# A trunk kernel on one core: weight loads issued strictly in program order, job additions two chunks later, and a unit's additions written between the high and the low part of its loaded sums

## Chip, cores and metric

The kernel runs on one core of a Trainium2 chip. The metric is the device time of one execution in microseconds (us). An engine's name in a profile stands for: PE the matrix engine, PEld its weight loads, DVE VectorE, ACT ScalarE, POOL GpSimd, SP SyncE (which here only issues DMA loads).

## The reference

An encoder trunk over 256 tokens of width 2048, batch 1, float32, two layers. Layer 0 mixes tokens by neighbourhood attention with 16 heads, layer 1 by a short gated convolution; each layer ends with a gated MLP of width 5632. Cut to what matters:

```python
h = x
for i in range(2):
    a = rms_norm(h, mix_norm[i])
    mixed = neighborhood_attention(a, ...) if i == 0 else short_conv_mixer(a, ...)
    h = h + mixed
    h = h + conv_glu_ffn(rms_norm(h, ffn_norm[i]), ...)
return rms_norm(h, final_norm)

# short_conv_mixer:  gb, gc, h = split(x @ w_in);  (gb * conv3(gc * h)) @ w_out
# conv_glu_ffn:      g, u = split(conv3(x @ w_up) + b);  (silu(g) * u) @ w_down
```

Nearly all of the work is x @ w with float32 weights, about 486 MB of them read once.

## The kernel before, in words

**Float32 by parts.** Every weight is split on the chip. A *chunk* is one load of 128x1024 float32 (512 KB) into a buffer `raw` (six buffers); ACT casts it to a high part `hi` (line 179), DVE subtracts that from the chunk to get the low part `lo` (line 180), six buffers each. PE then adds up three products: high x high, high x low, low x high.

**Two kinds of phase.** In a `Phase` (the projections into heads, `wqk`; into the MLP, `wup`; into the short convolution, `wsc`) weights are the stationary operand. A work item is a *pair* of output tiles of 128 features and four chunks; PE runs 32 matmuls on `hi` (line 251, with the activations' high and low parts beside each other, 512 columns), then 32 on `lo` (line 259, 256 columns). In a `Tokens` phase (`wo`, `wdown`, `wscout`) weights are the moving operand, three matmuls to a product (lines 442 to 444), and a work item is a *unit*: a plain one, or one with seven products in the place of eight, which needs sums of weights.

**What follows a pair.** The result of a `wup` tile leaves PSUM by: ACT copy (304), DVE addition (305), DVE product with the norm factor (310), ACT first tap of a convolution (318), two DVE taps (320), for the second tile of a pair silu on ACT (724), DVE product (727), ACT cast to the high part (283) and DVE subtraction (284). After some pairs GpSimd forms sums of the activations (lines 505 to 508), which ACT and DVE split again. A `wsc` tile goes the same way with lines 699, 702 and 316 in the place of 318, 724 and 727. A `wqk` pair gives q and k of a head; its scores (lines 596 to 598), softmax (603 to 611) and the transposes of its probabilities (621) follow some items later.

**Jobs.** A unit with seven products needs two sums of weight tiles that can be had ahead of time. A *job* (`make`) in an earlier `Phase` loads three tiles of 256 KB (lines 191 to 193) into activation buffers, later adds them (DVE, lines 198 and 199), and later still stores both sums to DRAM as `kept` (ACT's DMA queue, line 204). The unit loads them back as one chunk (line 146) and makes the last two sums from them on DVE (`pair_of_sums`, lines 159 and 160); ACT and DVE split those too (179, 180). There are 66 jobs and 66 such units. The lists `S_FIRST` to `S_ATT` say which units they are, `QK_JOBS` to `SC_JOBS` how many jobs each `Phase` takes, and `Phase.__init__` puts jobs between the first eighth and three quarters of its items.

**What sets the order.** `prep_to` walks the chunks some items ahead of PE (`AHEAD` = 4 chunks) and records each chunk's load, copy and subtraction. A job's additions and stores wait in `stores` for their chunk number:

```python
stores.append((len(prepped) + 4, adds))
stores.append((len(prepped) + 7, store))
```

The program is recorded in a layer that schedules it: from the recorded program it decides, engine by engine, in which order instructions stand, by its own reckoning of when each can begin; the place in the recorded program is a priority. `issue_after(x)` makes the instructions recorded inside it stand behind `x` on their engine. The order that results is fixed in the built program.

## Time and profile before

| what | value |
|---|---|
| median of 3 runs | 2222.01 us (2215.89 to 2222.76) |
| the profiled execution's own time | 2220.94 us |
| its span, first to last instruction | 2219.1 us |
| mean granted clock of PE | 0.997 |
| busy: PE, DVE, ACT, POOL | 99%, 84%, 58%, 5% of the span |
| DMA | mean 237 GB/s |

The span is what the profile divides; 1.8 us of the execution lie around it. A busy PE is drawn from modelled ends of its matmuls, so PE's share says that there are few gaps, not that it is at its peak. The clock that the throttle grants to PE is listed for every stretch of the span.

### The profile page before, as it was taken

Reading aid. Unit: us, or ns where it says so; the run is one execution under the profiler, and the core shown is the slowest. Engines: PE = TensorE matmul, PEld = TensorE weight load, DVE = VectorE, ACT = ScalarE, POOL = GpSimd, SP = SyncE. Lnnn points to the kernel's source line nnn. Section 1 sums busy time; section 2 is a strip of 40 time slices with the busy share of each in tenths; the row PEclk is TensorE's granted clock in tenths of the full one; section 3 lists DMA queues with packets and bytes.
Section 4 is the critical chain, followed back from the end, with each engine's and each line's share of the span. In section 5 each row is a group of like instructions: output and inputs, shape, how many; then the busy total and the mean of one; then the engine's idle time right before and its main releaser. Section 6 shows DMA issues by size and latency. Waiting matters only on the chain.

```text
span 2219.1 us, 33057 instructions
## 1 busy us (share of the span) xinstructions
PE 2190.1 (99%) x11710; PEld 1887.3 (85%) x11710; DVE 1853.0 (84%) x2856; ACT 1290.4 (58%) x1991; POOL 109.0 (5%) x159
## 2 busy tenths in 40 slices
PE   9999999999999999999999999999999999999998
PEld 8888888888888888887888888878888878888886
DVE  8788778888889888788887777888788989888888
ACT  7555555666665666565564455566556556566565
POOL 1011100000000000000000010000010000000000
PEclk9999999999999999999999999999999999999999
DMA  8799647777657788766698885677876667877575
GB/s 290 252 323 296 209 158 222 259 249 248 213 185 231 232 264 256 237 198 208 211 321 283 275 273 190 198 242 252 265 248 212 199 226 248 251 249 237 160 234 157
DMA packets 347670, 524.91 MB, mean 237 GB/s; under 512 B 19824, under 2 KB 250352, under 8 KB 347504
## 3 DMA queue, kind: packets, MB, share of 16 engines
q1 hardware_dynamic: 327120, 487.55, 68.9%
q10 hardware_dynamic: 20384, 35.24, 4.2%
q8 instruction: 92, 1.51, 0.3%
q14 instruction: 74, 0.61, 0.1%
HBM read 486.01 MB, written 36.70 MB: 236 GB/s over the span
## 4 chain that ended last, share of the span: by engine, by line
PE 73%; DVE 15%; issue 5%; ACT 3%; DMA 3%; SPq 0%; POOL 0%; ACTq 0%; DVEq 0%
PE mm L251 36%; PE mm L259 19%; DVE lo L180 7%; PE mm L444 3%; PE mm L443 3%; PE mm L442 3%; ACT hi L179 3%; DVE raw L160 1%; PE mm L668 1%; PE mm L670 1%; PE mm L669 1%; DVE raw L159 1%; DVE hi L180 1%; DMA act<-in_wdown 1%; DMA raw<-in_wup 1%
## 5 line engine op out<-in xcount | busy, mean ns | idle before, releaser
L180 DVE TENSOR_TENSOR lo<-raw,hi 128x1024 fp32r<-128x1024 f32 (+1 forms) x858 | 1020.3, 1214 | 121.4 <-ACT hi L179 70.7
L179 ACT CAST hi<-raw 128x1024 fp32r<-128x1024 f32 (+1 forms) x924 | 905.1, 1009 | 371.7 <-DVE raw L160 136.2
L251 PE MATMUL mm<-a,hi 128*128 128x512 f32 x4096 | 962.9, 391 | 2.0 <-DVE a L292 0.9
L251 PEld LDWEIGHTS mm<-a,hi 128*128 128x128 f32 x4096 | 759.7, 188 | 156.0 <-DVE a L292 2.2
L259 PEld LDWEIGHTS mm<-a,lo 128*128 128x128 f32 x4096 | 513.8, 192 | 14.2 <-DVE lo L180 2.4
L259 PE MATMUL mm<-a,lo 128*128 128x256 f32 x4096 | 519.9, 283 | 2.2 <-DVE lo L180 2.2
L442 PE MATMUL mm<-hi,act 128*128 128x512 f32 x624 | 245.0, 394 | 5.3 <-DVE h L339 2.1
L444 PE MATMUL mm<-hi,act 128*128 128x512 f32 x624 | 243.8, 391 | 0.0
L318 ACT ACTIVATE conv<-pad,pt 128x256 f32<-128x256 f32 x176 | 103.0, 599 | 207.7 <-DVE pad L310 199.5
L443 PE MATMUL mm<-lo,act 128*128 128x512 f32 x564 | 220.5, 391 | 0.0
L320 DVE SCALAR_TENSOR_TENSOR conv<-pad,pt,conv 128x256 f32<-128x256 f32 x384 | 178.3, 480 | 27.3 <-ACT conv L318 20.7
L304 ACT COPY corr<-mm 128x256 f32<-128x256 f32 x256 | 90.9, 370 | 159.6 <-PE mm L259 138.1
L442 PEld LDWEIGHTS mm<-hi,act 128*128 128x128 f32 x624 | 117.6, 188 | 33.2 <-ACT hi L179 5.0
L444 PEld LDWEIGHTS mm<-hi,act 128*128 128x128 f32 x624 | 117.4, 188 | 24.3
L443 PEld LDWEIGHTS mm<-lo,act 128*128 128x128 f32 x564 | 106.4, 189 | 22.1
L305 DVE TENSOR_TENSOR corr<-mm,corr 128x256 f32<-128x256 f32 x256 | 104.7, 417 | 10.4 <-ACT corr L304 10.2
L198 DVE TENSOR_TENSOR act<-act 128x512 f32<-128x512 f32 x66 | 45.9, 695 | 67.2 <-DMA act<-in_wdown 45.2
L284 DVE TENSOR_TENSOR act<-conv,act 128x256 fp32r<-128x256 f32 x88 | 40.1, 456 | 61.0 <-ACT act L283 61.0
L442 PE MATMUL mu<-hi,sf 128*128 128x512 f32 x186 | 73.5, 395 | 7.3 <-ACT hi L179 7.3
L443 PE MATMUL mu<-lo,sf 128*128 128x512 f32 x186 | 73.4, 395 | 1.1 <-DVE lo L180 1.1
L444 PE MATMUL mu<-hi,sf 128*128 128x512 f32 x186 | 72.5, 390 | 0.0
L310 DVE TENSOR_TENSOR pad<-corr,rstd 128x256 f32<-128x256 f32 x176 | 71.8, 419 | 0.1
(160 smaller groups left out, 1573.4 us busy)
## 6 DMA issues: line engine op xcount, KB each, us to landing
raw<-in_wup SPq DMA_DIRECT2D x352, 512.0 KB, 5.1
raw<-in_wdown SPq DMA_DIRECT2D x124, 512.0 KB, 4.4
raw<-in_wsc SPq DMA_DIRECT2D x96, 512.0 KB, 5.6
act<-in_wdown SPq DMA_DIRECT2D x156, 256.0 KB, 6.2
kept<-act ACTq DMA_DIRECT2D x132, 256.0 KB, 4.9
raw<-kept SPq DMA_DIRECT2D x66, 512.0 KB, 3.8
raw<-in_wqk SPq DMA_DIRECT2D x56, 512.0 KB, 5.6
raw<-in_wv SPq DMA_DIRECT2D x32, 512.0 KB, 4.8
```

What stands on the lines that cost most here:

```text
L179: newest["ACT"] = nc.scalar.copy(out=hv, in_=r)
L180: newest["DVE"] = nc.vector.tensor_sub(out=lv, in0=r, in1=hv.bitcast(F32))
L251: nc.tensor.matmul(self.ps[ft], lhsT=prepped[i][0][:, o:o + P], rhs=self.src[k], start=k == 0, stop=False)
L259: nc.tensor.matmul(self.ps[ft][:, S:], lhsT=prepped[i][1][:, o:o + P], rhs=self.src[k][:, :S], start=False, stop=k == self.nk - 1)
L304: nc.scalar.copy(out=corr, in_=ps[:, S:])
L305: nc.vector.tensor_add(out=corr, in0=ps[:, :S], in1=corr)
L310: nc.vector.tensor_mul(out=dst, in0=both(ps), in1=rstd)
L318: nc.scalar.activation(c, x[:, 1:S + 1], AF.Identity, scale=w[1], bias=b)
L320: nc.vector.scalar_tensor_tensor(out=c, in0=x[:, tap:tap + S], scalar=w[tap], in1=c, op0=ALU.mult, op1=ALU.add)
L442: nc.tensor.matmul(ps, lhsT=xh, rhs=wh, start=start, stop=False)
L443: nc.tensor.matmul(ps, lhsT=xh, rhs=wl, start=False, stop=False)
L444: nc.tensor.matmul(ps, lhsT=xl, rhs=wh, start=False, stop=stop)
```

## The change

Every load of weights, the jobs' included, goes through a new function `load`, which puts it behind the load recorded just before it on SP. Before, only the jobs' loads stood behind an earlier load. `parts` is split, so that a unit's last two sums are recorded between the high part (ACT) and the low part (DVE) of its loaded chunk. A job's additions are due six chunks after its loads in the place of four, its stores nine in the place of seven. Jobs begin at a fifth of the items where the `Phase` has single-tile items ahead, at once elsewhere (an eighth before), and end at three quarters, in the `wsc` phase at nine tenths.

```diff
-                newest["SP"] = nc.sync.dma_start(out=raw[:, :w], in_=src)
+                load(raw[:, :w], src)
...
             if kind == "kept":
-                newest["SP"] = nc.sync.dma_start(out=raw, in_=src())
-                t13 = parts(raw)
-                prepped.append((t13, parts(pair_of_sums(raw, prepped[-1][2], prepped[-2][2]))))
+                load(raw, src())
+                t13, low = high_part(raw)
+                t24 = pair_of_sums(raw, prepped[-1][2], prepped[-2][2])
+                low()
+                prepped.append((t13, parts(t24)))
...
+    def load(out, in_):
+
+        with ExitStack() as order:
+            if "SP" in newest:
+                order.enter_context(tc.issue_after(newest["SP"].ins))
+            newest["SP"] = nc.sync.dma_start(out=out, in_=in_)
...
+    def high_part(r):
...
         newest["ACT"] = nc.scalar.copy(out=hv, in_=r)
-        newest["DVE"] = nc.vector.tensor_sub(out=lv, in0=r, in1=hv.bitcast(F32))
-        return hi, lo
+
+        def low():
+            newest["DVE"] = nc.vector.tensor_sub(out=lv, in0=r, in1=hv.bitcast(F32))
+        return (hi, lo), low
...
-        stores.append((len(prepped) + 4, adds))
-        stores.append((len(prepped) + 7, store))
+        stores.append((len(prepped) + 6, adds))
+        stores.append((len(prepped) + 9, store))
...
-            made, lo, hi = 0, len(order) // 8, len(order) * 3 // 4
+            made, lo, hi = 0, len(order) // 5 if intro else 0, int(len(order) * until)
...
-    Phase(wsc, range(3 * KT), KT, a2, sc_evac, intro=3, jobs=take(SC_JOBS))
+    Phase(wsc, range(3 * KT), KT, a2, sc_evac, intro=3, jobs=take(SC_JOBS), until=0.9)
```

The changed file's lines from 156 on are some 9 higher (179 becomes 188, 180 becomes 191, 251 becomes 260, 304 becomes 313). All engines have the same instructions in both; what moved is their order, at three places above all.

**ACT, first `wup` phase, between two pairs.** Before: the pair on PE here is `mm_4877` and `mm_4894`, and the next is `mm_4998` and `mm_5015`, which reads `hi_4974`, `hi_4980` (both some rows above this piece), `hi_4986` and `hi_4994`; `hi_5088`, `hi_5094` and `hi_5102` belong to the pair after that. `corr` is the copy of a finished tile out of PSUM.

```order
L179 CAST hi_4986<-raw_4984 128x1024
L179 CAST hi_4994<-raw_4992 128x1024
L724 ACTIVATE g_4821<-conv_4817 128x256
L179 CAST hi_5088<-raw_5086 128x1024
L283 CAST act_4848<-conv_4843 128x256
L179 CAST hi_5094<-raw_5092 128x1024
L304 COPY corr_4927<-mm_4877 128x256
L304 COPY corr_4953<-mm_4894 128x256
L318 ACTIVATE conv_4931<-pad2_85,pt_79 128x256
L179 CAST hi_5102<-raw_5100 128x1024
L318 ACTIVATE conv_4957<-pad0_83,pt_79 128x256
L724 ACTIVATE g_4935<-conv_4931 128x256
```

All four copies for the next pair, and two for the one after, stand ahead of the first row that needs this pair's matmuls. The same pair in the changed program is `mm_4864` and `mm_4881`, and the next, `mm_4985` and `mm_5002`, reads `hi_4963` first, then `hi_4969`, `hi_4975` and `hi_4981`:

```order
L313 COPY corr_4914<-mm_4864 128x256
L327 ACTIVATE conv_4918<-pad2_85,pt_79 128x256
L313 COPY corr_4940<-mm_4881 128x256
L733 ACTIVATE g_4922<-conv_4918 128x256
L327 ACTIVATE conv_4944<-pad0_83,pt_79 128x256
L292 CAST act_4949<-conv_4944 128x256
L188 CAST hi_4963<-raw_4961 128x1024
L188 CAST hi_4969<-raw_4967 128x1024
L188 CAST hi_4975<-raw_4973 128x1024
L188 CAST hi_4981<-raw_4979 128x1024
```

Now all four copies for the next pair stand behind the whole evacuation of this one, down to the cast of its last activations. Counted over both programs, the first copy that an item needs stands behind a row that needs the last matmul of the item before it in no case before, and in 45 cases now: 33 in the `wup` phases (25 of them behind the cast of the activations as here, 7 behind the casts of GpSimd's sums as well, one behind the `conv` row), 10 in the `wsc` phase (5 right behind a `corr` copy, 2 behind the cast of the activations, 3 behind GpSimd's sums as well) and 2 in `wqk`.

**PE, `wqk` phase, second and third group of heads.** `sc` are the scores of a head, `tr` the transposes of its probabilities, which need the softmax of those scores. Before:

```order
L259 MATMUL mm<-a,lo 128x256 x16
L596 MATMUL sc<-qk 128x256
L597 MATMUL sc<-qk 128x256
L598 MATMUL sc<-qk 128x256
L596 MATMUL sc<-qk 128x256
L597 MATMUL sc<-qk 128x256
L598 MATMUL sc<-qk 128x256
L259 MATMUL mm<-a,lo 128x256 x16
L251 MATMUL mm<-a,hi 128x512 x32
L259 MATMUL mm<-a,lo 128x256 x16
L621 MATMUL tr<-pt,s 128x128 x4
```

Between the scores and the transposes stand 64 matmuls of the next pair. Now:

```order
L268 MATMUL mm<-a,lo 128x256 x16
L605 MATMUL sc<-qk 128x256
L606 MATMUL sc<-qk 128x256
L607 MATMUL sc<-qk 128x256
L605 MATMUL sc<-qk 128x256
L606 MATMUL sc<-qk 128x256
L607 MATMUL sc<-qk 128x256
L630 MATMUL tr<-pt,s 128x128 x4
L260 MATMUL mm<-a,hi 128x512 x32
```

The scores follow the last matmul of their own pair, and the transposes follow the scores with nothing between.

**DVE, a unit with seven products in the first `wdown` phase.** `raw_7653` is the loaded chunk of sums, `raw_7648` the tile in which the last two sums are made. In the changed program:

```order
L191 TENSOR_TENSOR hi_7650<-raw_7648,hi_7650 128x512
L191 TENSOR_TENSOR lo_7656<-raw_7653,hi_7655 128x1024
L167 TENSOR_TENSOR raw_7648<-raw_7653,raw_7648 128x512
L168 TENSOR_TENSOR raw_7648<-raw_7648,raw_7621 128x512
L191 TENSOR_TENSOR lo_7662<-raw_7648,hi_7661 128x1024
```

Nothing moved here: before, the same five rows stand in the same order (with lines 180, 159 and 160), and the low part `lo_7656` is still ahead of both additions. Over the 66 units, the low part stands ahead of both additions in 30 before and 28 now, between them in 16 and 16, behind both in 20 and 22; 64 units keep the order that they had.

## The prediction, as it was put on record before the changed kernel ran

> **What bounds the kernel now.** I read the page's busy times first, then what PE waited for, then the groups by line with shapes kept apart, then stretches around PE's longest waits.

> ```profile
> span 2219.1 us, 33057 instructions
> ...
> PE 2190.1 (99%) x11710; PEld 1887.3 (85%) x11710; DVE 1853.0 (84%) x2856; ACT 1290.4 (58%) x1991; POOL 109.0 (5%) x159
> ```

> PE is the bound throughout: nothing done on another engine shows in the time unless it makes PE wait, and every wait put in front of PE shows in full. PE's own waits in all:

> ```profile
> PE mu L442 <- ACT hi L179: 7.9, 12, 1.5
> PE mm L259 <- DVE lo L180: 2.2, 1, 2.2
> ...
> PE mm L251 <- ACT hi L179: 0.6, 3, 0.2
> ```

> The reader is to see the last row: in the `Phase` stages, where line 251 is the first matmul of a pair, PE waited 0.6 us in all for its high parts. There is almost nothing to gain there, and something to lose. The first row belongs to the units with seven products.

> Whether ACT can be late shows in a stretch of the `wsc` phase, by its waits:

> ```profile
> DVE act L198 <- DMA act<-in_wdown: 4.1, 1, 4.1
> ACT corr L304 <- DVE act L198: 3.7, 1, 3.7
> ...
> PE mm L259 <- DVE lo L180: 2.2, 1, 2.2
> ```

> A job's addition waited 4.1 us at DVE's head for its load; a store of those sums waited on ACT for the addition, and behind the store a copy `corr` stood 3.7 us that needed only PE. Each engine takes its list in order, and what stands behind a waiting row waits too; here it ended as 2.2 us on PE. By that reading the 45 places of the order at which a pair's first high part stands behind the evacuation of the pair before are 45 waits of PE.

> **The change part by part.** *The copies behind evacuations.* The rows of the chain, in time per instruction:

> ```profile
> L251 PE MATMUL mm<-a,hi 128*128 128x512 f32 x4096 | 962.9, 391 | 2.0 <-DVE a L292 0.9 <-DVE h L339 0.6 <-ACT hi L179 0.6
> L179 ACT CAST hi<-raw 128x1024 fp32r<-128x1024 f32 x842 | 862.0, 1047 | 360.6 <-DVE raw L160 136.2 <-PE mm L251 43.7 <-PE mm L444 39.0
> L259 PE MATMUL mm<-a,lo 128*128 128x256 f32 x4096 | 519.9, 283 | 2.2 <-DVE lo L180 2.2
> ...
> L320 DVE SCALAR_TENSOR_TENSOR conv<-pad,pt,conv 128x256 f32<-128x256 f32 x384 | 178.3, 480 | 27.3 <-ACT conv L318 20.7 <-ACT conv L316 3.6
> ...
> L305 DVE TENSOR_TENSOR corr<-mm,corr 128x256 f32<-128x256 f32 x256 | 104.7, 417 | 10.4 <-ACT corr L304 10.2
> L318 ACT ACTIVATE conv<-pad,pt 128x256 f32<-128x256 f32 x176 | 103.0, 599 | 207.7 <-DVE pad L310 199.5 <-DVE corr L305 7.8
> L304 ACT COPY corr<-mm 128x256 f32<-128x256 f32 x256 | 90.9, 370 | 159.6 <-PE mm L259 138.1 <-DVE corr L305 9.4 <-DVE act L198 6.9
> ...
> L310 DVE TENSOR_TENSOR pad<-corr,rstd 128x256 f32<-128x256 f32 x176 | 71.8, 419 | 0.1
> ...
> L727 DVE TENSOR_TENSOR conv<-conv,g 128x256 f32<-128x256 f32 x88 | 37.2, 423 | 5.2
> ...
> L283 ACT CAST act<-conv 128x256 fp32r<-128x256 f32 x88 | 35.3, 401 | 12.4 <-DVE conv L727 11.8
> ...
> L507 POOL TENSOR_TENSOR s<-conv,s 128x128 f32<-128x128 f32 x27 | 16.3, 603 | 2.1
> ...
> L505 POOL TENSOR_TENSOR s<-conv 128x128 f32<-128x128 f32 x27 | 14.3, 529 | 284.3 <-DVE conv L727 284.3
> ```

> From the pair's last matmul to the next pair's first high part: copy 0.37, addition 0.42, product 0.42, tap 0.60, two taps 0.96, product 0.42, cast 0.40, copy 1.05, together 4.64 us. One tap of the pair's first tile stands among these on DVE (0.48), and some nine hand-overs from engine to engine come to about 0.3. That is 5.4 us of PE with nothing to run. A bound from above is what the same chain took before, with other rows mixed in (ACT's timeline):

> ```profile
> 463.29 0.37 ACT L304 COPY corr<-mm 128x256 f32<-128x256 f32 x1 [1.55 <-PE mm L259]
> ...
> 469.76 0.40 ACT L283 CAST act<-conv 128x256 fp32r<-128x256 f32 x1
> 470.62 1.05 ACT L179 CAST hi<-raw 128x1024 fp32r<-128x1024 f32 x1 [0.46 <-ACT act L283]
> ```

> From 463.29 to 470.16, 6.87 us, and a copy more makes 7.9. The bounds are 4.6 and 7.9; I take 5.4, as the rows that were mixed in (`hi`, `lo`) stand behind the chain now.
> - `wup`, behind the cast: 25 x 5.4 = 135.0.
> - `wup`, behind GpSimd's sums: three GpSimd rows more (about 0.55 each) less the overlap with the cast: 1.6 more, 7 x 7.0 = 49.0.
> - `wup`, behind the `conv` row: 0.37 + 0.42 + 0.42 + 0.60 + 1.05 and 0.2 for hand-overs, 3.1.
> - `wsc`, right behind a `corr` copy: 0.37 + 1.05 and hand-overs, 5 x 1.7 = 8.5; behind the cast (copy, addition, two products, cast and copy at 0.37, 3 x 0.42, 0.40 and 1.05, two taps of the tile before, less their overlap) 2 x 4.2 = 8.4; behind GpSimd's sums too, 3 x 5.8 = 17.4.
> - `wqk`: scores wait for copy, addition, product, cast and subtraction (about 2.0), run for 0.7 (six matmuls of line 259's size at 519.9 / 4096 us), and the transposes wait for the softmax, whose rows are

> ```profile
> L603 DVE SCALAR_TENSOR_TENSOR s<-sc,bias 128x256 f32<-128x256 f32 x32 | 12.8, 414 | 0.0
> ...
> L608 ACT ACTIVATE s<-s,m 128x256 f32<-128x256 f32 x32 | 16.0, 501 | 7.1 <-DVE m L606 7.1
> ...
> L611 DVE TENSOR_SCALAR s<-s,z 128x256 f32<-128x256 f32 x32 | 11.3, 394 | 0.1
> L606 DVE TENSOR_REDUCE m<-s 128x2 f32<-128x512 f32 x16 | 10.8, 675 | 0.0
> ```

> two each of the first three and one of the last, 3.3, with small rows and hand-overs about 4.3: 6.5 without the 0.7 of work and rounded, twice, 13.0.

> Sum 135.0 + 49.0 + 3.1 + 34.3 + 13.0 = 234.4 us. What PE misses then cannot be made up, as it is the bound. Within such a pair the other three copies follow at 1.05 each, while eight matmuls of line 251 take 1.9 (962.9 / 4096 each): no second wait.

> *The clock.* Stretches around two of PE's waits, PE alone: busy time, matmuls, granted clock, DMA.

> ```profile
> 1276.00:1278.30 2.30, 0.13 (x2) 1.00 0.90 279
> 1278.35:1281.77 3.42, 3.42 (x13) 0.50 1.01 244
> 1281.77:1285.20 3.43, 3.43 (x17) 1.00 0.85 306
> ...
> 1046.50:1050.00 3.50, 2.09 (x9) 1.00 0.56 152
> 1050.00:1053.40 3.40, 3.18 (x15) 1.00 0.93 280
> ```

> After 2.17 us without work the clock fell to half for 3.42 us, which costs 1.7; 1.4 us without work left it whole. So gaps of 3 us and more should each bring one such stretch: 25 + 7 + 1 + 5 + 2 = 40 gaps x 1.7 = 68.0. The five of 1.7 us lie between the two rows; I give them nothing. Per gap the bounds are 0 and 3.4 (two stretches).

> [...]

> *Jobs' additions later.* The 132 additions and 132 stores are as many as before, two chunks later on DVE and ACT. The one wait of theirs that reached PE goes: 2.2 and its half clock of 1.7, 4.0 gained. What else DVE waited for them was covered by PE's matmuls.

> *Loads in order on SP.* The same loads; a chunk's load now also waits behind a job's three loads. Cover: the loads still stand more than most of a pair ahead, and a pair is 32 rows each of lines 251 and 259, 11.6 us, against a landing of about 5 us:

> ```profile
> raw<-in_wup SPq DMA_DIRECT2D x352, 512.0 KB, 5.1
> ...
> act<-in_wdown SPq DMA_DIRECT2D x156, 256.0 KB, 6.2
> ```

> I take 0. Without the cover each of the 52 jobs in `wup` and `wsc` would add up to 6.2.

> *Additions between a unit's parts.* 64 of 66 units keep DVE's order, so the 7.9 us of the unit's waits stay: 0, with bounds of -7.9 and, as the low part could come later by two additions in two units, +2.8.

> Sum: the profiled execution's 2220.9 (span 2219.1 and 1.8 around it) + 234.4 + 68.0 - 4.0 = 2519.3; the median stands 1.1 above that execution: 2520.

> **The rivals.**
> - *Not slower: ACT does not hold the copies back.* If a high part were cast as soon as its load has landed, whatever waits ahead of it, PE would find it done, and only the 4.0 are left: 2218. It decides at whether the copy ends before the pair's last `lo` matmul does, place by place. Against it: the 3.7 us row of `corr` behind another's wait. 4%, half of it faster if the units' 7.9 go too.
> - *The waits without the clock.* If gaps that return every 11 or 22 us leave the clock whole: 2452. For it: most short gaps did; against: the 0.50 row. 10%.
> - [...] 14%.
> - *Late loads on top.* If half of the 52 jobs add 3 us, as SP stands behind job loads whose buffers come free late, 2600. For it: DMA shares near 1.0 in the stretch above; against: the gaps give loads more time. 7%.

> **How the numbers follow.** Forecast 65%, the rivals 35%. The forecast's own range is 2480 to 2565 (chain 5.0 to 5.9, clock 1.2 to 2.2 a gap). The range over the cases, 2455 to 2570, leaves out the not-slower case, most of late loads and a part of the second. A difference of 0.3%, 6.7 us, is about what this kernel's runs can tell from none: faster 0.02, same 0.02, slower 0.96.

> **What the profile after would show.** PE's waits for ACT's `hi` in the first `hi` matmul of a pair go from 0.6 us to near 215 over some 43 waits, most between 5 and 7.5 us, in the `wup` and `wsc` phases; PE's busy share near 88%; the mean clock near 0.95 to 0.975; the stretch of 0.50 after most gaps; ACT waiting much longer for DVE's `pad` and product rows; the units' row at 6 to 9 us; DVE's waits for job loads gone. Wrong would be: fewer than 40 such waits, or waits of 2 us (then the order doesn't bind as read); a whole clock; new rows of ACT waiting for `raw` loads.

## The result, and the profile after

The changed kernel takes 2540.4 us (median of 4 runs, 2538.8 to 2542.4) against 2222.1: ratio 1.144, 95% interval 1.1417 to 1.1463. The forecast was 2520, slower. The page of the profiled execution, its own time 2542.4 us:

```profile
span 2540.6 us, 32802 instructions
...
PE 2291.6 (90%) x11710; PEld 1954.9 (77%) x11710; DVE 1885.4 (74%) x2856; ACT 1308.3 (51%) x1991; POOL 95.8 (4%) x159
```

The span is 321.5 us longer. PE's busy time accounts for 101.5 of that (2291.6 against 2190.1) with the same 11710 matmuls, its idle time for 220.0. What PE waited for (us in total, times, longest):

```profile
PE mm L260 <- ACT hi L188: 214.7, 45, 6.9
PE mu L451 <- ACT hi L188: 7.0, 11, 1.5
PE tr L630 <- DVE s L620: 6.9, 2, 3.5
PE sc L605 <- ACT qk L292: 3.6, 2, 1.8
```

The first row was 0.6 us in 3 waits. Of its 45 waits now, 43 (213.9 us) are at places counted from the order; the other two, at 9.0 and 836.1 us of the span, are 0.6 and 0.2 us long and were not. The two places in `wqk` show in the rows `tr` and `sc`, so that 45 of 45 places brought a wait. In each of the 43 the copy that PE waited for began at once behind the evacuation's row: ACT did not wait for a load there. One such wait on ACT, of those behind GpSimd's sums, in the first `wup` phase (start, duration, engine, line, work, and in brackets the idle time ahead):

```profile
458.15 0.41 ACT L292 CAST act<-conv 128x256 fp32r<-128x256 f32 x1 [1.03 <-DVE conv L736]
463.65 0.37 ACT L313 COPY corr<-mm 128x256 f32<-128x256 f32 x1 [5.09 <-PE mm L268]
...
469.33 0.40 ACT L292 CAST act<-conv 128x256 fp32r<-128x256 f32 x1 [1.53 <-DVE conv L736]
470.54 0.51 ACT L292 CAST sf<-s 128x384 fp32r<-128x384 f32 x1 [0.80 <-POOL s L515]
471.07 0.30 ACT L292 CAST act<-s 128x128 fp32r<-128x128 f32 x1
471.27 3.88 ACT L188 CAST hi<-raw 128x1024 fp32r<-128x1024 f32 x4
```

and on PE:

```profile
461.54 3.99 PE L268 MATMUL mm<-a,lo 128*128 128x256 f32 x32
472.37 2.08 PE L260 MATMUL mm<-a,hi 128*128 128x512 f32 x4 [6.83 <-ACT hi L188]
```

The four `hi` copies at 471.27 are those of the next pair. Their loads had been issued from 451.33 on, and the trace has them landed by 456.4, 458.2, 459.7 and 460.9. ACT had stood idle for 5.09 us with `corr` next in its list, until PE ended the pair: time for all four copies (4 x 1.05), had they stood ahead. Over the whole kernel this is a row of ACT's groups (busy us, mean ns, then idle before and what ended it), 138.1 of the idle time before, 505.2 now:

```profile
L313 ACT COPY corr<-mm 128x256 f32<-128x256 f32 x256 | 95.2, 372 | 515.2 <-PE mm L268 505.2 <-DMA act<-in_wscout 6.7 <-DMA kept<-act 1.5
```

The other part of the loss is the clock. Stretches of 3.41 us around the same wait, PE alone (busy time, matmuls, granted clock, DMA):

```profile
463.06:466.48 3.42, 2.47 (x21) 1.00 0.17 67
466.48:469.89 3.41, 0.00 (x0) 1.00 0.00 0
469.89:473.30 3.41, 0.93 (x2) 0.50 0.00 0
473.30:476.72 3.42, 3.42 (x9) 0.50 0.52 165
476.72:480.13 3.41, 3.41 (x16) 1.00 0.89 270
```

Two stretches at half clock follow one wait, the first of them partly still idle. In the whole record of the granted clock, the last 6 us of the span left out, there are 76 such stretches, 259.4 us, in which PE is at work for 196.2. At half clock a matmul on `hi` (line 260) started 0.427 us after the one ahead of it, at full clock 0.227 (medians over the changed kernel). I count half of PE's time at work there as lost, an estimate: 98.1 us (by these two steps it would be 47%). Before it was two stretches, 6.8 us, and by the same estimate 3.4 lost.

### The profile page after: what moved, and what is told of

Read it like the earlier page. It is cut to its first block, busy times and chain, and to the rows that moved or that the text cites. A ratio compares the mean times of both kernels' runs of the same rounds, so it can differ in the third digit from the quotient of the medians.

```text
span 2540.6 us, 32802 instructions
## 1 busy us (share of the span) xinstructions
PE 2291.6 (90%) x11710; PEld 1954.9 (77%) x11710; DVE 1885.4 (74%) x2856; ACT 1308.3 (51%) x1991; POOL 95.8 (4%) x159
## 4 chain that ended last, share of the span: by engine, by line
PE 77%; DVE 11%; ACT 7%; issue 3%; DMA 1%; POOL 0%; ACTq 0%; SPq 0%; DVEq 0%
PE mm L260 40%; PE mm L268 16%; PE mm L453 4%; PE mm L452 4%; PE mm L451 4%; ACT hi L188 3%; DVE lo L191 3%; DVE conv L329 2%; ACT conv L327 1%; PE mu L452 1%; PE mu L453 1%; PE mu L451 1%; DVE corr L314 1%; PE mm L678 1%; PE mm L679 1%
## 5 line engine op out<-in xcount | busy, mean ns | idle before, releaser
L260 PE MATMUL mm<-a,hi 128*128 128x512 f32 x4096 | 1057.4, 418 | 215.7 <-ACT hi L188 214.7
L191 DVE TENSOR_TENSOR lo<-raw,hi 128x1024 fp32r<-128x1024 f32 (+1 forms) x858 | 1009.4, 1212 | 211.5 <-ACT hi L188 104.6
L260 PEld LDWEIGHTS mm<-a,hi 128*128 128x128 f32 x4096 | 823.7, 204 | 402.8 <-ACT hi L188 225.6
L188 ACT CAST hi<-raw 128x1024 fp32r<-128x1024 f32 (+1 forms) x924 | 893.3, 1010 | 325.6 <-DVE raw L168 120.4
L268 PEld LDWEIGHTS mm<-a,lo 128*128 128x128 f32 x4096 | 513.0, 191 | 11.8
L313 ACT COPY corr<-mm 128x256 f32<-128x256 f32 x256 | 95.2, 372 | 515.2 <-PE mm L268 505.2
L327 ACT ACTIVATE conv<-pad,pt 128x256 f32<-128x256 f32 x176 | 105.8, 601 | 85.6 <-DVE pad L319 85.6
L292 ACT CAST act<-conv 128x256 fp32r<-128x256 f32 x88 | 35.5, 404 | 75.2 <-DVE conv L736 75.2
## 6 DMA issues: line engine op xcount, KB each, us to landing
raw<-in_wup SPq DMA_DIRECT2D x352, 512.0 KB, 5.7
raw<-in_wdown SPq DMA_DIRECT2D x124, 512.0 KB, 4.4
raw<-in_wsc SPq DMA_DIRECT2D x96, 512.0 KB, 6.1
act<-in_wdown SPq DMA_DIRECT2D x156, 256.0 KB, 5.9
kept<-act ACTq DMA_DIRECT2D x132, 256.0 KB, 3.9
raw<-kept SPq DMA_DIRECT2D x66, 512.0 KB, 4.1
raw<-in_wqk SPq DMA_DIRECT2D x56, 512.0 KB, 6.4
raw<-in_wv SPq DMA_DIRECT2D x32, 512.0 KB, 5.7
```

The source lines that it names most:

```text
L188: newest["ACT"] = nc.scalar.copy(out=hv, in_=r)
L191: newest["DVE"] = nc.vector.tensor_sub(out=lv, in0=r, in1=hv.bitcast(F32))
L260: nc.tensor.matmul(self.ps[ft], lhsT=prepped[i][0][:, o:o + P], rhs=self.src[k], start=k == 0, stop=False)
L268: nc.tensor.matmul(self.ps[ft][:, S:], lhsT=prepped[i][1][:, o:o + P], rhs=self.src[k][:, :S], start=False, stop=k == self.nk - 1)
L313: nc.scalar.copy(out=corr, in_=ps[:, S:])
L327: nc.scalar.activation(c, x[:, 1:S + 1], AF.Identity, scale=w[1], bias=b)
```

## Experiments

Theory A: the time is lost because ACT's copies for a pair stand behind the evacuation of the pair before, which the strict order of loads brings about. Rivals: B, the later additions or moved jobs do it; C, loads in strict order are late; D, the longer busy time is not the clock.

**The strict order undone, all else kept.**

```diff
-    def load(out, in_):
+    def load(out, in_, behind=False):
-            if "SP" in newest:
+            if behind:                 # True for the jobs' loads alone
                 order.enter_context(tc.issue_after(newest["SP"].ins))
```

> The changed kernel with one part undone: loads of chunks are no longer put behind the load recorded before them (the jobs' loads still are); later additions and stores, job spacing and the split unit stay. Theory A (the loss comes from ACT's order, which the strict order of loads brings about): no copy stands behind the evacuation of the pair before, PE's waits for hi in the phases fall from 214.7 us to under 3, the clock is near 0.997, and the time is 2218 us (2222 less the 4.0 of the one wait for a job's addition). Rival B (the later additions and stores, or the moved jobs, hold ACT and DVE up): the time stays within 20 us of 2540.

2216.1 us, ratio 0.9978 (0.9969 to 0.9987). The row of PE's waits for `hi` in the phases is down to 0.4 us in 2 waits; the clock is 0.998. B falls: additions, stores, job spacing and units are those of the changed kernel here.

**The strict order alone, added to the kernel before.** The order that `load` sets, and nothing else of the change.

> The kernel before with only the strict order of loads added; additions and stores of jobs four and seven chunks after their loads, old spacing, old units. Theory A: 43 copies behind evacuations instead of 45, waits of PE for hi in the phases near 210 us, half-clock stretches as in the changed kernel, time 2535 us (2520 to 2550). Rival B: 2222 us.

2528.2 us, ratio 1.1377 (1.1357 to 1.1397).

```profile
PE mm L260 <- ACT hi L188: 211.6, 43, 7.0
```

41 of these waits stand at places counted from the order (two others, 1.2 and 0.2 us, do not); with the two places in `wqk` that makes the 43 counted. One part of the change is thus both necessary and nearly sufficient for the loss.

**In order, but not behind jobs; and behind jobs only.** Two halves of the strict order, in the changed kernel:

```diff
# not behind jobs: a job's load waits for the newest chunk load, and no load waits for it
+            x = nc.sync.dma_start(out=out, in_=in_)
+        if not job:
+            newest["SP"] = x
# behind jobs only: jobs' loads, and the first chunk load after them
-            if "SP" in newest:
+            if job or was_job[0]:
                 order.enter_context(tc.issue_after(newest["SP"].ins))
+        was_job[0] = job
```

Expected of the first:

> The changed kernel, but a chunk's load stands behind the chunk load before it only, no longer behind a job's loads; a job's loads stand behind the last chunk load as before. Theory A, narrowed (what turns ACT's order is that a chunk's load is put behind a job's loads, for whose buffers the scheduler reckons a long wait): no copy behind an evacuation, 2218 us. Rival C (any strict order of loads on SP makes loads late): over 2400 us.

and of the second:

> The changed kernel, but only the first chunk load after a job stands behind the job's loads (and the jobs' loads behind the newest load, as in both kernels); the other chunk loads are free. Theory A, narrowed (that one order brings about all 45 places): 45 places, 2540 us (2530 to 2550). Rival: the strict order of the other loads is needed too, so that the later copies slip: under 2400.

2216.1 us, ratio 0.9977 (0.9967 to 0.9986), for the first, 2537.2 us, ratio 1.1425 (1.1401 to 1.1449), for the second. The second has the same 43 waits at the counted places, 213.7 us, and the two in `wqk`. What turns ACT's order is one relation: the first chunk load after a job is put behind that job's loads. Chunk loads in strict order among themselves cost nothing.

Why this relation makes the scheduler put the copies so late is not shown: its reckoning leaves no trace. A hint is that loads wait on SP for what they hardly waited for before. Their issues waited for the landing of an earlier job's store twice before, and 75 times in the changed kernel (SP's waits, of before and of after):

```profile
SPq L141 <- DMA kept<-act: 5.9, 2, 3.2
```
```profile
SPq L161 <- DMA kept<-act: 269.9, 75, 8.6
```

**Strictly in order, with the copies forced ahead.** This keeps every load where the change put it and moves only ACT's rows.

```diff
-                    self.evac(ft, self.ps.pop(ft))
+                    later_evac.append((self.evac, ft, self.ps.pop(ft)))   # pairs of wup and wsc
...
                 prep_to(ends[item[0]] + AHEAD)
+            for evac, f, ps in later_evac:
+                evac(f, ps)            # its corr copies stand behind newest["ACT"]
```

> The changed kernel with every load strictly in order as there, but the evacuation of a pair in the wup and wsc phases is recorded after the loads and copies of the next pair, and its corr copies are made to stand behind the newest of these copies on ACT. Theory A (ACT's order, not the loads, is what costs): of the 45 places five are left, which the edit does not reach (2 in wqk at 1.8 + 3.5 us, and the three pairs that follow single tiles, 3.0 + 1.6 + 4.9): 20 us, and some 7 half-clock stretches of 1.7: 2216 + 32 = 2248 us, 2235 to 2265. Rival C (loads in strict order come late behind the jobs' loads): copies wait for loads instead, over 2300.

2243.0 us, ratio 1.0102 (1.0086 to 1.0118), forecast 2248. The five places left are there with the sizes worked out (9.3 + 6.9 + 3.6 = 19.8 us), while the loads' waits on SP for those stores are longer than in the changed kernel (PE's waits, then SP's):

```profile
PE mm L260 <- ACT hi L188: 9.3, 3, 4.9
...
PE tr L637 <- DVE s L627: 6.9, 2, 3.5
PE sc L612 <- ACT qk L296: 3.6, 2, 1.8
```
```profile
SPq L161 <- DMA kept<-act: 327.0, 92, 9.7
```

So C falls: the loads' waits for stores are there in full, and PE does not notice. What the five places leave is near: 19.8 us of waits and an estimated 8.9 of half clock (half of 17.8 us of work there), 28.7, against 26.9 over the 2216.1 of the loads undone. The rest of the loss goes with ACT's order alone.

**The waits filled with idle matmuls.** At 38 of the 43 places in the row of `hi` (all but the five right behind a `corr` copy), on PE, ahead of the pair's first matmul:

```diff
+            with tc.issue_after(last[0].ins):          # the last matmul of the pair before
+                for i in range(n):                     # n from the size of the wait
+                    newest["PE"] = nc.tensor.matmul(x, lhsT=src[0][:, :P], rhs=src[1][:, :S],
+                                                    start=i == 0, stop=i == n - 1)
```

> The changed kernel with 16 to 48 idle matmuls (256 columns, 0.12 us each, results unused) put on PE at the start of 38 of the 45 pairs that wait, sized to fill the wait but for about 1 us; ACT's and DVE's orders are those of the changed kernel. Theory A (of the 321 us lost, about 220 are waits and about 100 the half clock after them): the waits' ends do not move, but the stretches at half clock after them go; mean clock above 0.985, time 2450 us (2435 to 2465). Rival D (the 100 us of longer busy time is not the clock but matmuls that follow their copies one by one, or slower because loads crowd in): 2520 to 2545 us. If the idle matmuls push the pairs behind them: above 2545.

2456.3 us, ratio 1.1056 (1.1037 to 1.1074), clock 0.994. PE does 1412 matmuls more (the group's row below) and the kernel is 84 us faster than the changed one. What is left of the waits stands in the second row.

```profile
L235 PE MATMUL st<-a 128*128 128x256 f32 x1412 | 175.5, 283 | 0.0
```
```profile
PE mm L275 <- ACT hi L188: 45.2, 45, 1.6
```

The half-clock stretches fall from 76 to 7 (23.9 us, PE at work for 16.2), which by the same estimate is worth (196.2 - 16.2) / 2 = 90 us. The idle matmuls and what is left of the waits come to 175.5 + 45.2 = 220.7, 6.0 more than the 214.7 that they stand for, and so 84 is left of the 90. D falls: PE's busy time without the idle matmuls is 2377.0 - 175.5 = 2201.5 us, where the changed kernel has 2291.6, 90.1 more, so the longer busy time was the clock. It also shows the prediction's second rival, the waits with a whole clock, priced at 2452.

**2.2 us left idle in each wait.** The same with 1007 idle matmuls in the place of 1412.

> As e4_gaps_filled, with fewer idle matmuls (5 to 38), so that about 2.2 us of each of the 38 waits is left without work in the place of 0.9. The waits end where they did; what differs between the rules is how many of the 38 bring a stretch at half clock. If the clock counts PE's work in windows of 3.41 us that run on freely, and a window with less than about half its time at work is followed by one at half clock (as the windows of the changed kernel and of e4 read): the 2.2 us must lie with at least 1.6 of it in one window, (3.41 + 2.2 - 3.2) / 3.41 = 70%, some 27 stretches of 1.7 us on top of 2456: 2502 us, 2490 to 2512. If any wait of 2 us and more brings one: 38, 2521. [...]

2476.7 us, ratio 1.1160 (1.1138 to 1.1182), below both forecasts, and 20.4 above the 2456.3 of the waits filled. Of the 38 waits with 2.0 us idle and more (at most 2.35) 18 brought a half-clock stretch in the profiled execution, not 27 and not 38. That execution took 2483.3 us at a clock of 0.983; the other three, 2475.1 to 2477.4 at 0.986, by that clock had some fewer. Where the border lies can be read from stretches of 3.41 us that begin where the clock's own steps lie, counted in steps of 3.413 us from a recorded change of the clock. Two of them, each with the one behind it:

```profile
867.42:870.83 3.41, 1.60 (x7) 1.00 0.00 0
870.83:874.24 3.41, 3.41 (x17) 1.00 0.74 219
2161.07:2164.48 3.41, 1.54 (x7) 1.00 0.01 2
2164.48:2167.89 3.41, 3.41 (x10) 0.50 0.71 226
```

1.60 us at work kept the clock, 1.54 did not. With a border just above 1.54 at work, 1.87 idle, I estimate the share of positions in which a wait of 2.2 us brings a half stretch at (3.41 + 2.2 - 3.74) / 3.41 = 55%, 21 of 38; my 1.6 came from stretches with other matmuls in them and was too low. What I foresaw holds in kind, with the border at 45 to 47% of a stretch at work; that every wait of 2 us brings one does not.

**The later additions alone.** Six and nine chunks in the kernel before (the diff's two lines).

> The kernel before with only the jobs' additions six and stores nine chunks after their loads. Prediction's step: the one wait of 2.2 us on PE at 1278 and its half clock go, 4.0 us: 2217 us, ratio 0.998. Rival: another stretch takes the wait's place: 2221, ratio 1.000.

2218.1 us, ratio 0.9982 (0.9973 to 0.9991): 2 to 6 us gained, against the 4.0 of the prediction. (In this run and the next two a job's three loads also stand in order among themselves; the next run has that too, and its time is that of the kernel before.) The waits did not go as the prediction had it. PE's wait of 2.2 us for a low part became three:

```profile
PE mm L268 <- DVE lo L191: 3.1, 3, 1.3
```

One of the two half-clock stretches went, an estimated 1.7 us; where the rest of the gain comes from is not shown. DVE still waited for the jobs' loads, 69.5 us before and 71.4 here, nearly all in the first of a job's two additions. With the strict order alone, the additions still due after four chunks, it did not (that first addition, here and there):

```profile
L207 DVE TENSOR_TENSOR act<-act 128x512 f32<-128x512 f32 x66 | 46.1, 699 | 71.6 <-DMA act<-in_wdown 47.5 <-DMA act<-in_wscout 19.3 <-DMA act<-in_wo 4.4
```
```profile
L207 DVE TENSOR_TENSOR act<-act 128x512 f32<-128x512 f32 x66 | 45.2, 684 | 0.0
```

**A unit's additions recorded between the parts, alone.** The diff's part in the `kept` branch.

> The kernel before, with only a unit's two additions recorded between the high and the low part of its loaded sums, nothing forced. Prediction's step: 64 of 66 units keep their order on DVE, no change: ratio 1.000, 2221. Rival: the two units that change (from the low part ahead to the low part behind) are among those at which PE waits, and up to 2 x 1.7 us go: ratio 0.9985.

Ratio 0.9997 (0.9986 to 1.0008). Recorded order is only a priority here; this part does nothing that can be measured.

**The same, forced.** In all 66 units, in the kernel before:

```diff
+                with tc.issue_after(newest["sum"].ins):    # the second of the two additions
                     low()
```

> The kernel before, where the low part of a unit's loaded sums is made to stand behind both additions on DVE (in all 66 units; the changed kernel left 28 of them with the low part ahead). If the low part ahead of the additions is what makes PE wait for the high part of the last two sums: of the 7.9 us (12 waits of up to 1.5) at least 5 go, 2216 us, ratio 0.9975. Rival: the low part, 1.4 us later, is now what PE waits for (line 452 in place of 451): 2221 or up to 2.8 above.

2202.6 us, ratio 0.9918 (0.9903 to 0.9932): about 18 us by that ratio, where I had counted on 5 to 8. First the groups of the kernel before, then of this one (busy us, mean ns, idle before):

```profile
L442 PE MATMUL mm<-hi,act 128*128 128x512 f32 x624 | 245.0, 394 | 5.3 <-DVE h L339 2.1 <-ACT hi L179 2.0 <-DVE corr L305 1.0
...
L442 PE MATMUL mu<-hi,sf 128*128 128x512 f32 x186 | 73.5, 395 | 7.3 <-ACT hi L179 7.3
L443 PE MATMUL mu<-lo,sf 128*128 128x512 f32 x186 | 73.4, 395 | 1.1 <-DVE lo L180 1.1
```
```profile
L452 PE MATMUL mm<-hi,act 128*128 128x512 f32 x624 | 243.5, 391 | 0.8 <-DVE h L349 0.8
...
L453 PE MATMUL mu<-lo,sf 128*128 128x512 f32 x186 | 72.5, 390 | 0.0
...
L452 PE MATMUL mu<-hi,sf 128*128 128x512 f32 x186 | 72.3, 390 | 0.3 <-ACT hi L189 0.3
```

Idle time shrinks by 12.6 in these three rows, and the span by 21.7 (2197.4). Matmul by matmul, from start to start, most of the difference lies at these lines, in two forms that the idle column doesn't have. In the kernel before, a matmul of these lines that waited started 0.39 us plus the idle time shown after the one ahead of it (0.48 in two of thirteen waits over 0.3 us), where the usual step was 0.227, so that each shown wait cost some 0.15 more; and the matmul behind it came 0.31 to 0.34 after it. The kernel's two half-clock stretches are one here.

**The best of both.** `load` as in the first experiment, and the unit's order forced as here.

> e1_loads_loose (later additions, moved jobs, loads of chunks not in strict order) with the low part of a unit's loaded sums behind both additions in all 66 units. If both gains are real and apart: 2216 less 5 to 7, 2210 us, ratio to before 0.995. If the unit's wait only changes its name: 2216, ratio 0.998.

2198.7 us, ratio 0.9900 (0.9886 to 0.9913): about 1% faster than the kernel before, and faster than the changed one. Against the forced unit alone its interval overlaps, so what the later additions add to it isn't shown.

## Why the prediction was right, point by point

**The copies behind evacuations: right, in number and size.** 45 places were counted from the order, and all 45 brought a wait of PE: 43 in the row of `hi`, two in `wqk`. By kind, forecast and measured: `wup` behind the cast 135.0 and 130.8 (25 of 5.2 us); behind GpSimd's sums 49.0 and 48.1 (7 of 6.9); behind `conv` 3.1 and 3.0; `wsc` right behind `corr` 8.5 and 7.7, behind the cast 8.4 and 7.8, behind GpSimd 17.4 and 16.6; `wqk` 13.0 and 10.5 (6.9 + 3.6). Together 234.4 and 224.5. The chain's lower bound of 4.64 plus hand-overs was the right end to take: the rows that were mixed into the chain before had indeed moved behind it.

**The clock: right in kind, too small.** The term was 68.0 (40 stretches of 1.7); busy time rose by 101.5. Mis-sized was the number of stretches per wait: one was taken, and of the 35 waits of 4.9 us and more 28 brought two, two three and five one. In the 35 stretches at half clock that another followed PE was idle for 0.61 us and more, in the 41 that a stretch at full clock followed for 0.52 and less. Over the 40 waits that is some 2.4 us each, above the 1.2 to 2.2 of the forecast's own range. As forecast, the five of 1.4 to 1.6 us behind a `corr` copy brought none. By the estimate above 98.1 - 3.4 = 94.7 us are the clock, and 45 times the hidden 0.15 of a wait is 6.8, together the 101.5. So 2520 fell 20 short: 10 too many in the waits, 33 too few here, and some 3 of small differences the other way. That the total came so near owes something to the two errors having opposite signs. The experiment with filled waits shows this term by itself, 84 us of it.

**Jobs' additions later: right in number, not in mechanism.** 4.0 forecast, 2 to 6 measured alone; but alone they left PE 3.1 us of such waits in the place of 2.2, and DVE its waits for jobs' loads, so that the agreement is in part luck. In the changed kernel no wait of DVE for a job's load is left, and the runs put that down to the strict order of loads: it is so with that order alone, and not with the additions alone.

**Loads in order on SP: right in price, and the step that mattered lay elsewhere.** The strict order is the cause of everything lost, but by way of ACT; the loads' own lateness cost PE nothing that shows (2216.1 us in order but not behind jobs; 2243.0 in order with the copies forced ahead, where the five places left account for 28.7). The prediction read the order of the copies and did not ask which part of the change had turned it.

**Additions between a unit's parts: right.** 0, measured 0.9997. The bound below, -7.9, was not a bound: made to happen, the order was worth about 18 us.

**The rivals.** Copies not held back: no. Waits without the clock, 2452: what the filled waits gave (2456.3), not what the change did, with its clock of 0.948. Late loads: no. Little idle time sufficed for a stretch at half clock: in the run with 2.2 us left idle 18 waits of at most 2.35 us brought one.

**What the profile would show.** 43 waits with 213.9 us against "some 43, near 215"; busy share 90% against 88%; clock 0.948, just under the range given; the unit's row 7.0, within 6 to 9. Two things were off. ACT waited longer for the product (75.2 us against 11.8), but shorter for `pad` (85.6 against 199.5): what grew most was its wait for PE's last `lo` matmul, ahead of `corr`. And ACT's waits for `raw` loads in `wup` grew from 13.3 us in 10 to 47.4 in 43, a sign named as one of being wrong; none of them stands right before a copy that PE waited for at the 43 places.

## What to carry to other kernels

An order that is asked of one queue can turn another engine's order, through the scheduler: read the built order of every engine before and after, and look for rows that a full engine needs early and that now stand behind rows that wait for that engine's end. Where a wait is left on PE, count the clock's stretches after it, here mostly two for a wait of 5 us, at some 2.4 us of loss together, and some 0.15 that the idle column hides. A preference given by the place in the program is no order; if it matters, force it, and measure, since here forcing it was worth more than the waits shown.
